# A two-layer mixer and expert trunk on one core: one layer's modulations computed on VectorE, S5 weights prepared later, the list check earlier, a new order

## The chip, the cores and the metric

The kernel runs on one core of one Trainium2 chip. The metric is the device time of one execution in microseconds (us); of several executions the median is given. Times of single instructions come from one execution that the hardware profiler recorded. PE is TensorE's matmul, PEld its weight load, DVE is VectorE, ACT is ScalarE, POOL is GpSimd, SP is SyncE, which here only issues DMAs.

## What is computed

512 tokens of width 1024 pass two layers. Each layer has a mixer and a mixture of experts:

```
mod = silu(c) @ ada_w[l] + ada_b[l]           # 6 vectors of 1024: shift, scale, gate, twice
h   = rms_norm(x) * (1 + sc1) + sh1
z   = h @ w_in[l]                             # columns go to four mixers
mix = concat(rwkv7(z), norm(s5(z)), norm(mla(z)), norm(rglru(z)))
x   = x + gt1 * (mix @ w_out[l])
h2  = rms_norm(x) * (1 + sc2) + sh2
x   = x + gt2 * moe(h2)                       # 32 experts, 2 per token: (silu(h2@w1) * (h2@w3)) @ w2
```

All of it is float32. `c` is one vector, so `mod` is a product of a vector with a 1024 x 6144 matrix: 24 MB of weights are read per layer for it. The experts' weights are 32 x 6 MB = 192 MB per layer, each read once.

## The kernel before

**Recording and planning.** The code does not issue instructions as it runs. `Rec` records each operation (so in the trace almost all of them have one line, L277), and `Rec.plan` then puts them in an order for each engine: it is a list scheduler with a cost per operation, limited by how many buffers of each kind there are. A step's `boost` adds to its priority. The tables `STEPS` (mixer steps, one string per layer, name and boost) and `MOE` (one tuple per layer: spacing of the experts and an offset for each of their stages) give these. Each engine runs its instructions strictly in the order that comes out.

**Names.** A tile's name is the part of the program that made it; a leading `q` is a PSUM tile. `ada` is the modulations, `z` the input norm and projection, `rw` and `rwc` RWKV, `s` S5, `mla` attention, `lru` the RG-LRU, `wo` the output projection and the running `x`, `n` the second norm and routing. Of the experts `moe_s` is the token list of a pair, `moe_g` the gathered tokens, `moe_h` the hidden layer, `moe_o` the outputs, and `moe_c` the combination, which adds them to `x` (tiles `wo`). `ct` is the constants, `pk` packed parameters, `r` the ring.

**Weights.** All large weights arrive by DMAs that SP issues in order. Ring tiles `r` hold 1 MB each, and there are six. Expert weights go partly into smaller tiles of 256 KB that the mixer uses for other things (`moe_h<-moe_w`, `moe_o<-moe_w`, called part tiles here); the list `OWN` says which of a layer's numbered loads do. The weights of the first experts can so arrive while the mixer still runs.

**Modulations.** `mod_chunk` handles 512 of the 6144 columns (chunks A0 to A11 for layer 0, A12 to A23 for layer 1; all 24 run before the end of layer 0's mixer). A chunk loads 2 MB into two ring tiles and issues 8 matmuls with `cond` (silu of `c`, padded with zero columns) as the stationary operand and 512 columns of weights moving: the 1024 inputs are 8 groups of 128 partitions, and four column groups of the PE array take a matmul each. `mod_cols` and `mod_rows` gather the four partial sums with small matmuls (`qada<-ct,ada`, `qada<-ada,ct`), and add the bias.

**S5 weights.** `s5w` computes layer 1's S5 matrices (powers, weights, frame; mostly VectorE with some matmuls `qs`) beside layer 0's experts. It is recorded after all experts with a very low priority, and may start once the first pair's tokens are gathered.

**Experts.** They run in 16 pairs, 64 slots per expert. Per pair: list, gather (a GpSimd DMA, transposes on PE, scaling on VectorE), hidden layer, outputs, combine. `outputs` scales the result on VectorE, rounds it on ScalarE (`oh`) and forms the remainder `ol` on GpSimd, so that `combine` can add both parts by matmuls with a 0/1 matrix.

**List check.** After the last pair's combine, `overflow` puts in a check: every engine reads whether an expert got more than 64 tokens, and branches (L2145 to L2167). With these inputs the branch is never taken. The planner treats it as a border that no recorded operation crosses.

**RWKV tiles.** `tile_a` builds a tile's decay matrices. Two products with the same stationary `Q` (against `BH`, 64 columns, and `AB`, 32 columns) are issued as separate matmuls.

Of the kernel before, what the change touches and what calls it, by code (L numbers as in the profile page):

```python
# [105 lines left out]
class Rec:  # L106


    def __init__(self, tc):
        self.tc, self.real = tc, tc.nc  # L110
        self.ops, self.hist, self.tag, self.cap = [], {}, {}, {}
        self.marks = []
        self.boost = 0.0
        self.after = None
        self.step = None
        self.stream = "main"
        self.nc = _Proxy(self)
# [9 lines left out]
    def add(self, eng, name, a, kw):  # L127
# [153 lines left out]
    def plan(self, seq, verbose=False):  # L281
# [28 lines left out]
        dma_free = hw_free = 0.0  # L310
# [16 lines left out]
        for si, (lo, hi) in enumerate(self.parts):  # L327
# [7 lines left out]
            while len(order) < hi - lo:  # L335
# [68 lines left out]
                free[e] = s + c  # L404
# [79 lines left out]
def _mk_consts():  # L484
# [25 lines left out]
    _const("selb", (p[:, None] % 32 == np.arange(4)[None, :]) | (p[:, None] == 4 + np.arange(4)[None, :]))  # L510
    _const("zero", np.zeros((1, 1)))
# [143 lines left out]
class Rwkv:  # L655
# [94 lines left out]
    def tile_a(self, tt):  # L750
# [26 lines left out]
        BH = k.s([128, 4, 64])  # L777
# [16 lines left out]
        ab2 = AB.rearrange("p h a t -> p h (a t)")  # L794
        nc.vector.tensor_mul(ab2, ab2, n2[:, tt, :, None].to_broadcast([128, 4, 2 * CH]))
# [47 lines left out]
        for at_, n, lhs, rhs, st in ((0, 64, lambda h, cs: Q[cs, h, 0], lambda h, cs: BH[cs, h], True),  # L843
                                     (64, CH, lambda h, cs: Q[cs, h, 0], lambda h, cs: AB[cs, h, 1], False),
# [11 lines left out]
        self.t[tt] = (CS, HS, AB, AK, Q, VB, MB, N, GT)  # L856

    def tile_b(self, tt, out):
# [5 lines left out]
        for hp in range(2):  # L864
            for h, i, ps_ in HS[hp::2]:
                for m, x in ((AB, Q[:, h, 1]), (AK, VB[:, h])):
                    for cs in CS:
                        nc.tensor.matmul(yp[hp][cs, i], m[cs, h, 1], x[cs], start=i == 0 and m is AB, stop=False,
                                         skip_group_check=True)
# [584 lines left out]
def positions(k, pool, pos):  # L1454
# [9 lines left out]
    for tt in range(4):  # L1464
# [15 lines left out]
MOE = [(133, 63, -18, 106, -205, -65, 19), (45, 33, 33, 167, 329, 46, 18)]  # L1480
# [134 lines left out]
class Trunk:  # L1615
# [115 lines left out]
    def mod_cols(self, l, g):  # L1731
# [5 lines left out]
        for j in range(4):  # L1737
            nc.tensor.matmul(pc[:, j], part[:, j::4], k.c("sel")[:, :g.n], start=True, stop=True)
# [6 lines left out]
    def mod_rows(self, l, g):  # L1745
# [8 lines left out]
        nc.tensor.matmul(pb[0:4], k.c("selb"), part, start=True, stop=True)  # L1754
# [289 lines left out]
    def hidden(self, xg, e, w13, gs, hd):  # L2044
# [4 lines left out]
        for j in range(8):  # L2049
# [3 lines left out]
            for q, ps in ((0, ph[os_]), (1, ph[es])):  # L2053
                nc.tensor.matmul(ps, xg[j][:, es], w[q][jj][0], start=j == 0, stop=j == 7, skip_group_check=True)
# [4 lines left out]
    def outputs(self, l, hd, w2):  # L2059
# [8 lines left out]
        for j in range(4):  # L2068
            if j % 2 == 0:
                w = [w2(e, j // 2) for e in range(2)]  # L2070
            for h in range(2):
                for e in range(2):
                    es = slice(64 * e, 64 * e + 64)
                    nc.tensor.matmul(po[h][es], hT[:, j, es], w[e][j % 2][h], start=j == 0,
                                     stop=j == 3, skip_group_check=True)
        out = []
        for h in range(2):
# [3 lines left out]
            self.split(of, nc.scalar, nc.gpsimd, oh, ol)  # L2081
# [13 lines left out]
    def moe(self, l, X, Z, E):  # L2095
# [8 lines left out]
        for e in range(0, E_N, 2):  # L2104
# [4 lines left out]
            if e == 0:  # L2109
                self.first = self.R.last.idx  # L2110
# [200 lines left out]
```

## Time and profile before

| | us |
|---|---|
| median of 3 executions (lowest, highest) | 1909.92 (1909.84, 1913.19) |
| profiled execution, its own time | 1914.02 |
| its span from first to last instruction | 1912.3 |
| PE busy | 1728.6 (90%) |
| DVE busy | 1002.4 (52%) |
| ACT busy | 430.3 (22%) |
| POOL busy | 145.5 (8%) |

The granted clock of TensorE was 0.938 of full speed over the span. The span has these stages, by the names in the timeline: a start of some 40 us; the mixer of layer 0 to about 458; its experts to about 1020; the mixer of layer 1 to about 1390; its experts to 1904; and the final stores. "Busy" of an engine in a window counts only instructions that compute. DMA is the share of the core's 16 DMA engines' time, GB/s what they moved. Idle time of PE is named after what ended it ("<-DMA" a transfer, "<-DVE z" a VectorE result).

### The profile page before, as it was taken

How to read it: one execution, taken by the hardware profiler on the slowest of the kernel's cores; microseconds unless marked ns; L12 is line 12 of the kernel's file. 1: busy time of each engine (PE TensorE's matmuls, PEld its weight loads, DVE VectorE, ACT ScalarE, POOL GpSimd, SP SyncE). 2: the span in 40 equal slices, each digit the busy share in tenths (PEclk: the TensorE clock that was granted, in tenths of full speed). 3: DMA queues.
4: the chain of work that ended last, by engine and by line, in shares of the span. 5: the costliest groups of instructions: out<-in, count | busy, mean ns of one | idle time of the engine just before them, and what ended most of it. 6: DMA issues, size and time to landing. Idle time of an engine off the chain costs nothing. (4 is left out here: it accounts for less than half of the span.)

```text
span 1912.3 us, 32680 instructions
## 1 busy us (share of the span) xinstructions
PE 1728.6 (90%) x12548; PEld 925.6 (48%) x12549; DVE 1002.4 (52%) x3448; ACT 430.3 (22%) x887; POOL 145.5 (8%) x136
## 2 busy tenths in 40 slices
PE   5989998897999998899897999999879998899987
PEld 2745655676344443333335765677734443333332
DVE  7966555658875543122226486677744374222312
ACT  3513234532011101010104253435301100100100
POOL 0000000001101220010100000000021141010101
PEclk9998998697999999999998999699989999999999
DMA  9384555044999988999995212114289999999996
GB/s 364 134 316 172 199 174 197 27 141 130 340 404 401 378 305 293 347 402 404 405 388 222 88 49 69 54 48 141 95 302 402 403 399 392 404 402 403 402 402 265
DMA packets 177397, 519.36 MB, mean 272 GB/s; under 512 B 18368, under 2 KB 20928, under 8 KB 147792
## 3 DMA queue, kind: packets, MB, share of 16 engines
q1 hardware_dynamic: 160272, 481.27, 66.3%
q10 hardware_dynamic: 11840, 19.13, 3.0%
q0 software_dynamic: 5120, 16.78, 2.6%
q8 instruction: 101, 1.65, 0.4%
q14 instruction: 64, 0.52, 0.1%
HBM read 508.71 MB, written 8.40 MB: 270 GB/s over the span
## 5 line engine op out<-in xcount | busy, mean ns | idle before, releaser
L277 PE MATMUL qmoe_h<-r,moe_g 128*64 128x512 f32 x1168 | 471.7, 608 | 17.5 <-DMA r<-moe_w 14.9
L277 PE MATMUL qmoe_h<-moe_h,moe_g 128*64 128x512 f32 x880 | 393.9, 604 | 1.5 <-DMA moe_h<-moe_w 1.5
L277 PE MATMUL qmoe_o<-r,moe_o 128*64 128x512 f32 x544 | 239.1, 647 | 16.1 <-ACT moe_o L277 14.6
L277 PEld LDWEIGHTS qmoe_h<-r,moe_g 128*64 128x64 f32 x1168 | 134.6, 139 | 201.1 <-issue 171.2
L277 DVE TENSOR_TENSOR wo<-qmoe_c,wo 128x512 f32<-128x512 f32 x256 | 159.9, 683 | 131.7 <-PE qmoe_c L277 131.6
L277 PE MATMUL qmoe_o<-moe_o,moe_o 128*64 128x512 f32 x480 | 224.9, 641 | 0.1
L277 PE MATMUL qz<-z,z 128*128 128x512 f32 (+1 forms) x816 | 216.1, 414 | 8.2 <-DVE lru L277 3.4
L277 PEld LDWEIGHTS qz<-z,z 128*128 128x128 f32 (+1 forms) x816 | 151.3, 192 | 60.3 <-issue 16.2
L277 ACT ACTIVATE moe_h<-qmoe_h 64x512 f32<-64x512 f32 x64 | 37.9, 592 | 570.5 <-PE qmoe_h L277 484.3
L277 DVE SCALAR_TENSOR_TENSOR moe_g<-qmoe_h,moe_s,moe_h 64x512 f32<-64x512 f32 x64 | 47.9, 749 | 221.6 <-ACT moe_h L277 218.8
L277 PEld LDWEIGHTS qmoe_h<-moe_h,moe_g 128*64 128x64 f32 x880 | 110.1, 138 | 104.3 <-issue 75.4
L277 PE MATMUL qmoe_c<-moe_o,moe_g 128*128 128x512 f32 x512 | 145.5, 415 | 13.7 <-ACT moe_o L277 7.9
L277 DVE TENSOR_TENSOR moe_o<-qmoe_o,moe 128x512 f32<-128x512 f32 x64 | 44.1, 691 | 211.6 <-PE qmoe_o L277 188.1
L277 POOL TENSOR_TENSOR moe_o<-moe_o,moe_o 128x512 fp32r<-128x512 f32 x64 | 82.6, 1298 | 799.4 <-ACT moe_o L277 641.1
L277 PEld LDWEIGHTS qmoe_c<-moe_o,moe_g 128*128 128x128 f32 x512 | 89.3, 188 | 101.3 <-issue 37.8
L277 PEld LDWEIGHTS qmoe_o<-r,moe_o 128*64 128x64 f32 x544 | 69.6, 147 | 137.6 <-issue 110.4
L277 POOL DMA_INDIRECT moe_g<-xn,moe_s x64 | 61.7, 964 | 946.5 <-DVE moe_s L277 857.4
L277 PE MATMUL qrw<-rw,rw 32*32 32x32 f32 (+6 forms) x4128 | 113.9, 220 | 7.3 <-DVE rw L277 2.0
L277 DVE TENSOR_SCALAR moe_g<-qmoe_g,A,B 128x128 f32<-128x128 f32 x256 | 85.5, 404 | 60.5 <-PE qmoe_g L277 47.1
L277 PEld LDWEIGHTS qrw<-rw,rw 32*32 32x32 f32 (+3 forms) x4128 | 82.0, 118 | 66.1 <-issue 26.8
L277 DVE TENSOR_TENSOR s<-s,s 128x128 f32<-128x128 f32 (+8 forms) x446 | 103.3, 290 | 3.7 <-ACT s L277 2.8
L277 ACT CAST moe_o<-moe_o 128x512 fp32r<-128x512 f32 x64 | 39.6, 619 | 282.6 <-DVE moe_o L277 209.3
(225 smaller groups left out, 2051.2 us busy)
## 6 DMA issues: line engine op xcount, KB each, us to landing
r<-moe_w SPq DMA_DIRECT2D x214, 1024.0 KB
moe_h<-moe_w SPq DMA_DIRECT2D x440, 256.0 KB
moe_o<-moe_w SPq DMA_DIRECT2D x240, 256.0 KB
r<-ada_w SPq DMA_DIRECT2D x48, 1024.0 KB
r<-w_in SPq DMA_DIRECT2D x16, 1024.0 KB
r<-w_out SPq DMA_DIRECT2D x8, 1024.0 KB
xn<-n ACTq DMA_DIRECT2D x16, 256.0 KB
z<-x SPq DMA_DIRECT2D x8, 256.0 KB
```

The costliest lines, as they stand in the source:

```text
L277: getattr(getattr(self.real, o.eng), o.fn)(*o.a, **o.kw)
```

## The change

1. Layer 1's modulations: a chunk's 8 matmuls become 8 VectorE operations 128x512 (one multiplication by a per-partition scalar, seven multiply-and-adds) into a tile `acc`, and one matmul with a matrix of ones sums the 128 partitions. Layer 0's chunks stay as they were.
2. `ada_w` is laid out on the host so that each partition's 8 KB of a ring tile lie together (four pieces of 2 KB before).
3. `tile_a`: `BH` and `AB` lie side by side in `BA`, and one matmul of 96 columns takes the place of one of 64 and one of 32; a ScalarE copy and a split VectorE operation per tile fill `BA`.
4. `s5w` is recorded after experts 18, 20 and 22, each part not before the combine of that pair, with that step's priority.
5. The list check stands ahead of the last pair's combine, in both layers, and the last pair's `ol` is formed on VectorE.
6. `OWN` sends loads 6 to 15 (instead of 6 to 11) and every odd one after them to part tiles.
7. The final stores go half to SP, half to ACT.
8. The planner takes the DMAs as free from 2.5 us on, does not hold SP at the list check, and lets a pair of matmuls wait for both weight tiles at once (`also`); `STEPS` and `MOE` have new numbers, so that all steps stand in a new order.

```diff
@@ Rec.plan
-        dma_free = hw_free = 0.0
+        dma_free, hw_free = 2500.0, 0.0
...
-                free[e] = s + c
+                if o.a is not None:
+                    free[e] = s + c
@@ tile_a
-        BH = k.s([128, 4, 64])
+        BA = k.s([128, 4, 64 + 2 * CH])
+        BH = BA[:, :, :64]
...
+        nc.vector.tensor_mul(AB[:, :, 0], AB[:, :, 0], n4)
+        nc.vector.tensor_mul(BA[:, :, 64:64 + CH], AB[:, :, 1], n4)
+        nc.scalar.copy(BA[:, :, 64 + CH:], AK[:, :, 1])
...
-        for at_, n, lhs, rhs, st in ((0, 64, lambda h, cs: Q[cs, h, 0], lambda h, cs: BH[cs, h], True),
-                                     (64, CH, lambda h, cs: Q[cs, h, 0], lambda h, cs: AB[cs, h, 1], False),
+        for at_, n, lhs, rhs, st in ((0, 64 + CH, lambda h, cs: Q[cs, h, 0], lambda h, cs: BA[cs, h, :64 + CH], True),
@@ tables
-MOE = [(133, 63, -18, 106, -205, -65, 19), (45, 33, 33, 167, 329, 46, 18)]
+MOE = [(134, 188, -31, 184, -340, -50, 357), (66, -306, 138, 370, 114, 93, -14)]
-OWN = [[i for i in range(6, 170) if i < 12 or i % 2] for _ in range(2)]
+OWN = [[i for i in range(6, 170) if i < 16 or i % 2] for _ in range(2)]
-STEPS = {0: """A0:7 A1:86 L1:72 A2:44 A3:194 G0 L4:56 G1 n:3 z1:-21 L0:104 L2:-12 A12 Z4:2 A8:-11 A9:3 w0:5 w1:2 A4:6 A5 A10:-4
+STEPS = {0: """A0:144 w0:3 L1:1 A2:-12 A3:22 A1:38 G0:-15 L2 G1:395 n:-30 z1:58 k:-37 L4:88 L0:23 Z4:-44 z2:203 A4:-21 w2:-362
...
@@ mod_chunk
+        w = self.early.pop((l, c), None) or self.load_ada(l, c)
+        if l:
+            acc = self.k.s([128, 512])
+            for h in range(2):
+                for q in range(4):
+                    col = self.cond[:, 4 * h + q, 3:4]
+                    if h + q == 0:
+                        nc.vector.tensor_scalar(acc, w[h][:, q], col, None, op0=OP.mult)
+                    else:
+                        nc.vector.scalar_tensor_tensor(acc, w[h][:, q], col, acc, op0=OP.mult, op1=OP.add)
+            g.acc[r] = acc
+            if r ^ 1 in g.acc:
+                if g.ps is None:
+                    g.ps = self.k.ps("d")
+                for n in (r & 2, r | 1):
+                    nc.tensor.matmul(g.ps[32 * n:32 * n + 32], self.k.c("ones")[:, :32], g.acc[n], start=True, stop=True)
+            return
@@ outputs
-            self.split(of, nc.scalar, nc.gpsimd, oh, ol)
+            self.split(of, nc.scalar, lo, oh, ol)
@@ moe
+            last = e == E_N - 2
+            out = self.outputs(l, hd, lambda q, h: self.load_w2(l, e + q, h), nc.vector if last else nc.gpsimd)
+            if last:
+                self.R.step, self.R.boost = None, 0.0
+                self.overflow(l, X, Z, G)
             stage(e, 5)
             self.combine(X, PT, out)
+            if e in between:
+                stage(e, 5)
+                self.R.after = self.R.last.idx
+                between[e]()
+                self.R.after = None
@@ store_x
-                self.nc.scalar.dma_start(dst[tt * 128:tt * 128 + 128, 512 * h:512 * h + 512], X[tt][h])
+                eng = self.nc.sync if h and dst is self.out else self.nc.scalar
+                eng.dma_start(dst[tt * 128:tt * 128 + 128, 512 * h:512 * h + 512], X[tt][h])
@@ build
-                self.R.after, self.R.boost = self.first, -4e6
-                for n in range(3 * (l + 1 < layers)):
-                    self.s5w(l + 1, n)
-                self.R.after, self.R.boost = None, 0.0
-                self.overflow(l, X, Z, G)
+                between = {18+2*n: partial(self.s5w, l + 1, n) for n in range(3)} if l + 1 < layers else {}
+                self.moe(l, X, Z, E, G, between)
@@ pack
+    ada = np.ascontiguousarray(np.asarray(a["ada_w"]).reshape(2, 2, 128, 4, 12, 512).transpose(0, 4, 1, 2, 3, 5))
```

The first place is layer 0's mixer. On PE before, modulation matmuls (`qada<-r,cond`) with their waits for ring DMAs stand between projection matmuls (`qz`) and attention (`qmla`):

```order
L277 MATMUL qada_184<-r_357,cond 32x512 [waits DMAHW4_49]
L277 MATMUL qada_184<-r_357,cond 32x512 x3
L277 MATMUL qada_184<-r_358,cond 32x512 [waits DMAHW5_49]
L277 MATMUL qada_184<-r_358,cond 32x512 x3
L277 MATMUL qada_184<-r_359,cond 32x512 [waits DMAHW6_49]
L277 MATMUL qada_184<-r_359,cond 32x512 x3
L277 MATMUL qada_184<-r_360,cond 32x512 [waits DMAHW7_49]
L277 MATMUL qada_184<-r_360,cond 32x512 x3
L277 MATMUL qada_284<-r_361,cond 32x512 [waits DMAHW0_49]
```

On PE after, at a place among the RWKV matmuls (`qrw`), one matmul with ones (`qada<-ada,ct`) is left of a chunk, and waits for VectorE:

```order
L279 MATMUL qrw_537<-rw_503,rw_532 64x96 [waits PE_49]
L279 MATMUL qrw_537<-rw_503,rw_532 64x96 x3
L279 MATMUL qrw_537<-rw_532,rw_503 64x64 x4
L279 MATMUL qrw_537<-rw_501,rw_504 64x64 x4
L279 MATMUL qada_294<-ada_333,ct 32x512 [waits DVE_49]
L279 MATMUL qz_411<-z_181,z_409 128x512
L279 MATMUL qz_411<-z_185,z_409 128x512
```

On DVE after, in the same stretch, the sums `ada` stand between RWKV operations (`rw`) and the splits of `w_in` (`z<-r`):

```order
L279 TENSOR_TENSOR rw_523<-qrw_522,ct 128x128 [waits PE_49]
L279 TENSOR_TENSOR rw_495<-qrw_494,rw_346 128x512
L279 TENSOR_SCALAR ada_333<-r_331,cond 128x512 [waits DMAHW4_49]
L279 TENSOR_SCALAR rw_495<-rw_495,pk_71 128x512 [waits DVE_49]
L279 STREAM_TRANSPOSE rw_526<-qrw_524 128x128 [waits Activation_49]
L279 SCALAR_TENSOR_TENSOR ada_333<-r_331,cond,ada_333 128x512 [waits DVE_49]
L279 TENSOR_TENSOR rw_528<-qrw_527,ct 128x128 [waits PE_49]
L279 TENSOR_TENSOR rw_503<-qrw_502,rw_496 128x4x64 [waits PE_49]
L279 SCALAR_TENSOR_TENSOR ada_333<-r_331,cond,ada_333 128x512 [waits DVE_49]
L279 TENSOR_TENSOR z_409<-r_327,z_407 128x512
L279 SCALAR_TENSOR_TENSOR ada_333<-r_331,cond,ada_333 128x512 [waits DVE_49]
```

So the sums share VectorE's queue with the chain on which the RWKV matmuls wait; the waits for ring DMAs moved with them.

The second place is layer 0's experts. On PE before, the S5 matmuls (`qs`) stand among the output matmuls of the seventh pair (`qmoe_o`) and the transposes of the last pairs' gathered tokens (`qmoe_g`):

```order
L277 MATMUL qmoe_g_1903<-ct,moe_g_1901 128x128 [waits DMASW4_49,DVE_49,PE_49]
L277 MATMUL qmoe_g_1903<-ct,moe_g_1901 128x128 x3
L277 MATMUL qs_2298<-s_2255,s_2273 32x32 [waits DVE_49,PE_49]
L277 MATMUL qs_2298<-s_2255,s_2273 32x32 x2
L277 MATMUL qmoe_o_1675<-r_1682,moe_o_1674 64x512 [waits DMAHW0_49]
L277 MATMUL qmoe_o_1676<-r_1682,moe_o_1674 64x512
L277 MATMUL qmoe_o_1675<-moe_o_1683,moe_o_1674 64x512 [waits DMAHW1_49]
L277 MATMUL qmoe_o_1675<-r_1682,moe_o_1674 64x512
L277 MATMUL qmoe_o_1676<-moe_o_1684,moe_o_1674 64x512 [waits DMAHW2_49]
```

On PE after, they stand inside the hidden layer (`qmoe_h`) of the twelfth pair, with waits on VectorE:

```order
L279 MATMUL qmoe_h_2057<-moe_h_2062,moe_g_2052 64x512 [waits DMAHW7_49]
L279 MATMUL qmoe_h_2057<-r_2063,moe_g_2054 64x512 [waits DMAHW0_49]
L279 MATMUL qs_2008<-s_1916,s_1934 32x32 [waits DVE_49]
L279 MATMUL qs_2008<-s_1916,s_1934 32x32 x3
L279 MATMUL qs_2008<-s_2007,s_1935 32x32 [waits DVE_49]
L279 MATMUL qs_2008<-s_2007,s_1935 32x32 x3
L279 MATMUL qs_2008<-s_1916,s_1936 32x32 x4
L279 MATMUL qs_2008<-s_2007,s_1937 32x32 x4
L279 MATMUL qs_2024<-s_1916,s_1934 32x32 [waits DVE_49]
L279 MATMUL qs_2024<-s_1916,s_1934 32x32 x3
```

The number of `qs` matmuls is the same. The last `qmoe_g` stands ahead of the sixth pair's outputs now, and the VectorE operations of `s5w`, which before began beside the first pairs, follow the combine of the tenth.

The third place is the end of layer 0's experts. On PE before, the last combine (`qmoe_c`) is followed by the read of the list count:

```order
L277 MATMUL qmoe_c_2245<-moe_o_2241,moe_g_2217 128x512 [waits Pool_49]
L277 MATMUL qmoe_c_2247<-moe_o_2241,moe_g_2217 128x512
L277 MATMUL qmoe_c_2249<-moe_o_2241,moe_g_2217 128x512
L277 MATMUL qmoe_c_2251<-moe_o_2241,moe_g_2217 128x512
L2145 TENSOR_LOAD cnt_85 [waits DVE_49]
L2146 COMPARE_AND_BRANCH
```

On PE after, the first row is the check's last branch, and the last combine follows it:

```order
L2187 UNCONDITIONAL_BRANCH [waits PE_49,PE_sequencer_49]
L279 MATMUL qmoe_c_2382<-moe_o_2379,moe_g_2353 128x512 [waits DVE_49,Activation_49]
L279 MATMUL qmoe_c_2382<-moe_o_2380,moe_g_2353 128x512
L279 MATMUL qmoe_c_2384<-moe_o_2379,moe_g_2353 128x512 [waits DVE_49,PE_49]
L279 MATMUL qmoe_c_2384<-moe_o_2380,moe_g_2353 128x512
L279 MATMUL qmoe_c_2386<-moe_o_2379,moe_g_2353 128x512
L279 MATMUL qmoe_c_2386<-moe_o_2380,moe_g_2353 128x512
```

What stood ahead of the border (combine, and on DVE the sums into `wo`) stands behind it, so that operations of the next layer's mixer can be mixed with it.

## Rows read from the trace of the kernel before

**Rows 1.** The page's first part: engine, busy us (share of the span) xinstructions.

```profile
PE 1728.6 (90%) x12548; PEld 925.6 (48%) x12549; DVE 1002.4 (52%) x3448; ACT 430.3 (22%) x887; POOL 145.5 (8%) x136
```

**Rows 2.** Windows by stage: length, busy per engine (x instructions), granted clock, DMA share, GB/s.

```profile
core 0: us, PE busy (x) PEld busy (x) DVE busy (x) ACT busy (x) POOL busy (x), PEclk, DMA share, GB/s
40.00:455.00 415.00, 391.49 (x4326) 260.21 (x4323) 267.15 (x1008) 156.76 (x334) 0.00 (x0) 0.92 0.49 172
1025.00:1385.00 360.00, 335.94 (x3868) 252.62 (x3868) 256.10 (x934) 151.30 (x331) 0.00 (x0) 0.90 0.26 92
485.00:690.00 205.00, 197.81 (x909) 81.54 (x907) 135.93 (x527) 20.24 (x35) 31.00 (x27) 0.99 1.02 389
690.00:800.00 110.00, 96.88 (x454) 41.22 (x451) 38.86 (x83) 11.55 (x24) 14.36 (x13) 0.95 0.83 290
800.00:1005.00 205.00, 184.89 (x732) 70.69 (x729) 47.39 (x73) 19.22 (x32) 15.32 (x12) 0.98 1.02 399
1410.00:1890.00 480.00, 443.85 (x1910) 181.89 (x1908) 165.51 (x352) 46.24 (x77) 59.08 (x52) 0.96 1.03 401
```

**Rows 3.** Groups of PE's and DVE's instructions by form: count, busy us, mean ns, idle before.

```profile
L277 PE MATMUL qada<-r,cond 128*32 128x512 f32 x384 | 69.1, 671 | 27.0 <-DMA r<-ada_w 13.6 <-ACT cond L277 13.3
...
L277 PE MATMUL qrw<-rw,rw 32*64 32x32 f32 x256 | 13.7, 216 | 0.0
...
L277 DVE SCALAR_TENSOR_TENSOR rw<-rw,pk,rw 128x512 f32<-128x512 f32 x4 | 3.0, 740 | 0.0
...
L277 DVE TENSOR_SCALAR rw<-rw,pk,rw 128x512 f32<-128x512 f32 x4 | 2.2, 543 | 1.2 <-PE qs L277 1.2
```

**Rows 4.** PE's waits in layer 0's mixer: total us, times, longest.

```profile
PE qada L277 <- DMA r<-ada_w: 10.0, 7, 5.0
PE qrw L277 <- issue: 1.9, 2, 1.5
```

**Rows 5.** Windows of 10 us in layer 0's experts, columns as in rows 2.

```profile
690.00:700.00 10.00, 10.00 (x42) 3.39 (x39) 1.93 (x6) 0.00 (x0) 2.59 (x3) 0.78 0.59 200
740.00:750.00 10.00, 8.36 (x26) 3.38 (x27) 1.80 (x3) 1.24 (x2) 2.56 (x2) 1.00 0.61 218
770.00:780.00 10.00, 6.03 (x22) 2.40 (x24) 0.76 (x1) 1.18 (x2) 0.00 (x0) 0.98 1.00 371
```

**Rows 6.** The same for instructions of the S5 tiles alone (PE: matmuls that read them).

```profile
500.00:520.00 20.00, 0.00 (x0) 0.00 (x0) 12.77 (x89) 0.42 (x2) 1.00 1.02 379
680.00:740.00 60.00, 5.89 (x144) 4.06 (x144) 0.00 (x0) 4.30 (x12) 0.94 0.82 292
```

**Rows 7.** SP's timeline ahead of the two expert stages: start, us, DMAs.

```profile
419.83 23.76 SPq L277 DMA_DIRECT2D moe_o<-moe_w  x16
481.65 0.33 SPq L277 DMA_DIRECT2D r<-moe_w  x1
...
1317.30 42.32 SPq L277 DMA_DIRECT2D moe_o<-moe_w  x16
1402.61 0.33 SPq L277 DMA_DIRECT2D r<-moe_w  x1
```

**Rows 8.** Timeline of all engines where layer 0's experts end: start, us, [idle before <-releaser].

```profile
1015.14 2.54 POOL L277 TENSOR_TENSOR moe_o<-moe_o,moe_o 128x512 fp32r<-128x512 f32 x2 [29.02 <-ACT moe_o L277]
...
1017.03 4.92 DVE L277 TENSOR_TENSOR wo<-qmoe_c,wo 128x512 f32<-128x512 f32 x8 [1.77 <-PE qmoe_c L277]
...
1019.63 8.49 SPq L277 DMA_DIRECT2D r<-w_in  x6
...
1027.12 1.96 PE L277 MATMUL qz<-ct,z 128*128 128x128 f32 x8 [7.62 <-DVE z L277]
```

**Rows 9.** Timeline of the last 20 us, columns as in rows 8.

```profile
1899.18 1.29 POOL L277 TENSOR_TENSOR moe_o<-moe_o,moe_o 128x512 fp32r<-128x512 f32 x1 [2.22 <-ACTq L2146]
...
1901.06 2.48 DVE L277 TENSOR_TENSOR wo<-qmoe_c,wo 128x512 f32<-128x512 f32 x4 [0.22 <-PE qmoe_c L277]
1903.64 4.53 ACTq L277 DMA_DIRECT2D out<-wo  x8
```

More of the change, by code (lines that the diff above doesn't have):

```diff
@@ L114, in __init__ @@
         self.after = None
+        self.also = ()
         self.step = None
@@ L137, in add @@
         rd += [x.ap for x in ins if isinstance(x, bass.IndirectOffsetOnAxis)]
+        rd += self.also
         if name == "matmul" and not kw.get("start", True):
@@ L867, in tile_b @@
                     for cs in CS:
-                        nc.tensor.matmul(yp[hp][cs, i], m[cs, h, 1], x[cs], start=i == 0 and m is AB, stop=False,
+                        nc.tensor.matmul(yp[hp][cs, i], m[cs, h], x[cs], start=i == 0 and m is AB, stop=False,
                                          skip_group_check=True)
@@ L1683, in load_ada @@
     def load_ada(self, l, c):
-        w = self.a["ada_w"][l].rearrange("(h p j) n -> h p j n", h=2, j=4)
-        return [self.ring(w[h, :, :, c * 512:c * 512 + 512], (4, 512)) for h in range(2)]
+        return [self.ring(self.a["ada_w"][l, c, h], (4, 512)) for h in range(2)]
     def load_win(self, l, q):
@@ L1737, in mod_cols @@
         for j in range(4):
-            nc.tensor.matmul(pc[:, j], part[:, j::4], k.c("sel")[:, :g.n], start=True, stop=True)
+            nc.tensor.matmul(pc[:, j], part[:, j::4], k.c("par" if l else "sel")[:, :g.n], start=True, stop=True)
         for r, (c, out, scale) in enumerate(g.out):
@@ L1753, in mod_rows @@
         pb = k.ps("d")
-        nc.tensor.matmul(pb[0:4], k.c("selb"), part, start=True, stop=True)
+        nc.tensor.matmul(pb[0:4], k.c("parb" if l else "selb"), part, start=True, stop=True)
         row = k.s([4, 512])
@@ L2053, in hidden @@
             for q, ps in ((0, ph[os_]), (1, ph[es])):
+                self.R.also = [w[1][jj][0]] if q == 0 else ()
                 nc.tensor.matmul(ps, xg[j][:, es], w[q][jj][0], start=j == 0, stop=j == 7, skip_group_check=True)
@@ L2073, in outputs @@
                     es = slice(64 * e, 64 * e + 64)
+                    self.R.also = [w[1][j % 2][h]] if e == 0 else ()
                     nc.tensor.matmul(po[h][es], hT[:, j, es], w[e][j % 2][h], start=j == 0,
@@ L2093, in combine, with moe @@
                 nc.vector.tensor_tensor(X[tt][h], ps, X[tt][h], op=OP.add)
-    def moe(self, l, X, Z, E):
+    def moe(self, l, X, Z, E, G, between):
+        nc = self.nc
         self.stream(f"moe{l}")
@@ L2108, in moe @@
             PT, xg = self.gather(l, tok, idx)
-            if e == 0:
-                self.first = self.R.last.idx
             hd = self.k.s([128, 512])
@@ L2135, in direct @@
         k = self.k
-        old = (self.nc, k.nc, k.sp, k.pp, self.live)
+        old = (self.nc, k.nc, k.sp, k.pp, self.live, self.own)
         self.nc = k.nc = self.R.real
-        k.sp, k.pp, self.live = self._Direct(self.sp, self.bufs), self._Direct(self.pp, self.pbufs), True
+        k.sp, k.pp, self.live, self.own = self._Direct(self.sp, self.bufs), self._Direct(self.pp, self.pbufs), True, []
         fn()
-        self.nc, k.nc, k.sp, k.pp, self.live = old
+        self.nc, k.nc, k.sp, k.pp, self.live, self.own = old
+        self.R.also = ()
     def over(self, l, X, Z, G):
@@ L2172, in over @@
                             self.hidden(xg, q, w13, gs, hd)
-                        out = self.outputs(l, hd, w2)
+                        out = self.outputs(l, hd, w2, nc.vector)
                         self.combine(X, PT, out)
@@ L2205, in setup @@
         nc.gpsimd.memset(self.cond, 0.0)
+        self.R.boost = 1e7
         nc.scalar.activation(self.cond[:, :, 3], ct, AF.Silu)
+        self.R.boost = 0.0
         self.cos, self.sin = positions(k, self.cp, a["pos"])
@@ L2225, in mods @@
             g = Group()
-            g.out, g.n = out, len(out)
+            g.out, g.n, g.ps, g.acc = out, len(out), None, {}
             chunks += [partial(self.mod_chunk, l, x[0], g, r) for r, x in enumerate(out)]
```

37 lines of the change are left out of this document (18 added, 19 removed).

## The prediction

> **What bounds the kernel now.** I read the page's first part, then a table of windows by stage, then PE's waits and groups inside each stage, and last the timeline at the two seams. The first part shows PE busy 90% of the span, DVE 52%, ACT 22%, POOL 8% [rows 1]. This is an average over stages with different limits, which the windows take apart [rows 2].
>
> In layer 0's mixer (40 to 455) PE is busy 391.5 of 415 us, DVE 267.2, and the DMAs at a share of 0.49. In layer 1's mixer (1025 to 1385) PE is busy 335.9 of 360. The two mixers differ mainly by the 24 modulation chunks, and the time differs as PE's work does: 55.6 us of PE, 55 us of span. So a mixer is bound by PE, with some 24 us of waits in each.
>
> The experts are another matter. From 1410 to 1890 the DMAs run at a share of 1.03 and 401 GB/s. A pair's weights are 12 x 1,048,576 = 12.58 MB, so 31.4 us at that rate; the 6.5 pairs that 800 to 1005 holds at this pace cost PE 184.9 us, 28.4 each [rows 2]. So experts are bound by DMA where nothing disturbs them. In layer 0 something does: from 690 to 800 only 290 GB/s flow, so 110 x (1 - 290/401) = 30.4 us of transfer are lost. [...] Layer 1's experts, which have no S5 weights beside them, show no such dip at 401 GB/s.
>
> **The change part by part.** The durations are from the profiled execution, 1914.0 us with a span of 1912.3; the median of the runs is 1909.9, 4.1 below it.
>
> *Modulations on VectorE.* The `qada<-r,cond` records are 384 with 69.1 us for both layers [rows 3]; half go: -34.6 us of PE. In their place come 12 ones-matmuls, 24 records of the same form. With four side by side, as now, one costs 69.1/384 = 0.18 us, so 4.3 in all; alone 0.671, so 16.1. They come two at a time: I take 8. DVE gets 84 multiply-and-adds at 0.740 and 12 multiplications at 0.543 (the same operations on SBUF tiles of 128x512): 62.2 + 6.5 = 68.7 us [rows 3]. DVE's idle time in the stage is 415 - 267 = 148 us [rows 2], which hides them if they fall into it. DVE would then be busy 336 of some 400 us, 84%, and its queue is in order: a sum in front of an operation on which the RWKV matmuls wait delays PE by up to 0.74 us. Waits for the ring move too: PE waits 10.0 us for `ada_w` in 7 places [rows 4], and in the second half of them DVE will stand in its stead, with rw operations and splits of `w_in` queued behind.
>
> *`tile_a`.* The 32-column matmuls (256 records, 13.7 us, so 6.9 per layer [rows 3]) go; the 96-column form that takes them in is not in the trace. Between nothing gained and 6.9 per layer I take 3.4. The 8 ScalarE copies lie in ACT's idle time (157 of 415 us busy [rows 2]).
>
> Together PE loses 34.6 - 8 + 3.4 = 30 us of work in layer 0's mixer. The gain in time lies between -35 (all of it, and half of the 10 us of waits) and a loss of 39 (68.7 of sums fully on the path, less 30). I take -14, about half of PE's gain, because DVE at 84% in order cannot hide everything. Layer 1's mixer: -3 (0 to -7).
>
> *S5 weights later.* In layer 0's experts, S5 takes DVE 12.8 of 20 us at 500 to 520, early, when lists and gathers of all pairs also want DVE; its matmuls fall on PE at 680 to 740 with 5.9 us [rows 6], beside the last gathers: the dip. From 485 to 690 DVE is busy 135.9 of 205 us and PE 197.8; from 800 to 1005 DVE is busy only 47.4 and PE has 20 us free [rows 2]. The change puts S5 there, behind all gathers. If the stage then looks like layer 1's, the 30.4 us come back; if the dip only moves, nothing. PE's late work has to be done in any case and is 96.5% busy ahead of the dip, so I take -19.
>
> *Deeper prefetch.* SP's part loads end at 443.6 and 1359.6, and its next ring load is issued at 481.65 and 1402.61 [rows 7]: 38 and 43 us without weights. 16 more part tiles are 4.2 MB, 10.5 us at 401 GB/s, in each layer. All of it would give -21. But at the start of the experts PE, at 96.5%, is as much the limit as the DMAs, so weights that lie ready are worth less: -6 (0 to -21). If the mixer holds the tiles longer, SP waits at them and the loads queued behind wait too; that end is 0, since SP stands still there today.
>
> *List check earlier.* At the seam GpSimd's two remainders take 2.54 us, the sums 4.92, SP's `w_in` loads come at 1019.63 after the last combine, and the first matmul of the next layer at 1027.12 waits on DVE [rows 8]. Remainders on DVE cost some 0.7 each. The loads can leave sooner, but the norm needs the sums in any case, so I take -2 (0 to -7). The added wait on DVE is behind the last scaling, with only the combine queued after it.
>
> *End.* Eight store issues take ACT 4.53 us in a row; in two queues 2.3 less. A remainder of 1.29 us on GpSimd is on the last chain, about 0.6 less on DVE [rows 9]. I take -3 (-1 to -5).
>
> *`ada_w`'s layout, the order.* PE's waits for `ada_w` bound the first at 0 to -5 together with the above; I take 0. The new order has no price of its own in the trace; PE's idle time in the mixers, some 24 us each, bounds what it can give, and I count none.
>
> Sum: -14 - 3 - 19 - 6 - 2 - 3 = -47, so 1867 against the profiled execution and 1863 against the median. I forecast 1865.
>
> **Rivals.**
>
> *VectorE eats the gain of the mixer.* For it: 84% busy, in order. Against it: 148 us idle now, and sums are not urgent. Then -14 is 0: 1879.
>
> *The dip only moves.* S5's matmuls on PE wait for DVE inside a hidden layer, and PE's queue behind them waits too. For it: 5.9 us of PE and its waits come in a stage with only 20 us of PE's idle time. Against it: DVE is nearly free there. Then -19 is 0: 1884.
>
> [...]
>
> *Slower: VectorE's queue becomes the path.* In layer 0's mixer nearly every sum stands ahead of an operation that PE awaits, and the sums' waits for the ring (10 us as PE had) hold DVE. Then 68.7 + 10 - 30 = +49 in place of -14: 1865 + 63 = 1928. It decides from +35 in this stage on, that is, when over 55 of the 68.7 us with the waits are on the path.
>
> *All ends at their best.* Mixer -35, dip -30, prefetch -21: 1865 - 21 - 11 - 15 = 1818.
>
> **How the numbers follow.** Forecast 0.42, VectorE eats the gain 0.14, the dip moves 0.12, the clock 0.07, all at their best 0.12, slower 0.10, and 0.03 that losses through the new order just cancel the gains. A difference of 0.2% (3.8 us) is about what a measurement of this kernel can tell from none. Slower has 0.10, no change 0.05 (the 0.03 and the edge of the slower case), faster 0.85. The range reaches from 1832, between forecast and best case, to 1898, above the rivals that cost one term or both (1865 + 14 + 19 = 1898); it leaves out the slower case and half of the best.
>
> **What would show it.** In layer 0's mixer, PE's busy time near 361 us over a stage some 14 us shorter; DVE near 336. If PE waits on DVE `rw` for more than 20 us there, the first or the slower rival holds. In layer 0's experts, windows of 10 us at 400 GB/s throughout, as in layer 1's; a dip where `qs` runs says that it moved. SP's pause before each expert stage begins with 4.2 MB more landed. At the seam the first `qz` comes 10.1 us after the start of the last sums today [rows 8]; it should come some 8 after it. The prediction is wrong if the mixer of layer 0 grows, or if neither expert stage gets shorter.

## The result and the profile after

The changed kernel takes 1858.46 us (median of 4, 1857.69 to 1869.05); before took 1909.88 beside it (median of 4, 1905.98 to 1913.19). By the medians that is 51 us less. The ratio is 0.9744, 95% interval 0.9705 to 0.9784, which makes it 49 us less, between 41 and 56. I forecast 1865, with 1832 to 1898 as the range. The total was near; the terms were not all, and one cause was not in the list at all, so that the nearness is in part luck.

Between the starts and ends of named matmuls in the two profiled executions (spans 1912.3 and 1856.6 us) the stages take:

| stage, us | before | after | moved | forecast |
|---|---|---|---|---|
| start and layer 0's mixer, to the last `qn` | 465.8 | 442.8 | -23.0 | -14 |
| `qn` to the first `qmoe_h`, both layers | 20.3 | 22.6 | +2.3 | |
| layer 0's experts, to the end of the last `qmoe_o` | 538.5 | 515.2 | -23.3 | -19, and part of -6 |
| from there to layer 1's first `qz` | 12.7 | 18.4 | +5.7 | -2 |
| layer 1's mixer | 357.6 | 350.2 | -7.4 | -3 |
| layer 1's experts | 502.8 | 493.2 | -9.6 | part of -6 |
| combine, sums, stores | 14.6 | 14.1 | -0.5 | -3 |

The moves add up to -55.8, more than the 51 of the medians, since the profiled execution of before took 1914.0, 4.1 above its median. A stage also varies from one profiled execution to the next: in the runs below that leave a stage's order and work alone, layer 0's mixer takes 462.1 to 467.9 us with before's order and 436.8 to 442.8 with the changed one, layer 0's experts 530.8 to 538.5 and 515.2 to 519.3. A few us in one stage of one trace therefore show nothing.

First the page's busy times, then the windows of the stages, as in [rows 1, 2]. PE lost 55 us, DVE gained 60.

```profile
PE 1673.4 (90%) x12124; PEld 900.2 (48%) x12125; DVE 1062.0 (57%) x3556; ACT 427.1 (23%) x891; POOL 139.3 (8%) x132
```

```profile
core 0: us, PE busy (x) PEld busy (x) DVE busy (x) ACT busy (x) POOL busy (x), PEclk, DMA share, GB/s
40.00:440.00 400.00, 378.25 (x4061) 260.76 (x4053) 332.25 (x1169) 156.27 (x339) 0.00 (x0) 0.90 0.51 189
1000.00:1340.00 340.00, 314.39 (x3702) 237.81 (x3700) 242.24 (x855) 136.74 (x306) 0.00 (x0) 0.93 0.26 89
...
660.00:770.00 110.00, 99.18 (x429) 38.09 (x426) 26.65 (x41) 11.81 (x20) 8.91 (x7) 0.97 1.03 416
770.00:970.00 200.00, 179.47 (x832) 68.28 (x831) 95.39 (x396) 22.20 (x44) 14.46 (x12) 0.97 0.92 361
...
900.00:910.00 10.00, 10.00 (x42) 4.79 (x42) 2.29 (x4) 0.89 (x2) 1.29 (x1) 1.00 0.64 243
```

In layer 0's mixer DVE is busy 332 of 400 us, as forecast (336), and PE 378 (361 forecast); the clock is 0.90. The stretch that ran at 290 GB/s in the middle of the experts [rows 2, 5] has 416 now. That is more than the 401 GB/s at which before ran undisturbed, and nothing in the prediction accounts for it.

The groups of PE and DVE by form, to be held against [rows 3]:

```profile
L279 DVE SCALAR_TENSOR_TENSOR ada<-r,cond,ada 128x512 f32<-128x512 f32 x84 | 60.5, 741 | 0.0
L279 DVE TENSOR_SCALAR ada<-r,cond 128x512 f32<-128x512 f32 x12 | 5.7, 475 | 1.8 <-PE qz L279 1.8
...
L279 PE MATMUL qada<-r,cond 128*32 128x512 f32 x192 | 33.2, 699 | 16.1 <-DMA r<-ada_w 16.1
L279 PE MATMUL qrw<-rw,rw 32*64 32x64 f32 x512 | 24.0, 238 | 0.0
L279 PE MATMUL qrw<-rw,rw 32*64 32x96 f32 x256 | 20.6, 277 | 1.3 <-DVE rw L279 0.8 <-ACT rw L279 0.6
...
L279 PE MATMUL qada<-ada,ct 128*32 128x512 f32 x24 | 13.2, 679 | 0.0
```

The sums cost DVE 66.2 us (forecast 68.7), the removed matmuls were 35.9 (34.6), the ones-matmuls are 13.2 (8).

PE's largest waits in that mixer (40 to 440), where [rows 4] had 10.0 us for `ada_w`. There is none for `ada_w` now, whose 16.1 us above lie ahead of 40, and none for the sums `ada` among the first:

```profile
PE qrw L279 <- DVE rw L279: 5.0, 5, 1.8
PE qz L279 <- ACT rw L279: 3.4, 1, 3.4
```

Instructions of the S5 tiles alone in layer 0's experts (columns as in [rows 6]). S5 now runs from 760 to 880 beside transfers at 380 to 415 GB/s, and the late low stretch (205 GB/s) has none of it:

```profile
780.00:800.00 20.00, 0.00 (x0) 0.00 (x0) 10.99 (x80) 0.42 (x2) 0.83 1.01 393
820.00:840.00 20.00, 2.66 (x76) 2.06 (x76) 11.24 (x37) 3.59 (x11) 1.00 1.03 415
900.00:920.00 20.00, 0.00 (x0) 0.00 (x0) 0.00 (x0) 0.00 (x0) 1.00 0.57 205
```

In the late stretch PE is full (10.00 of 10 us from 900 to 910, above) and SP waits for it to free ring tiles (from 870 to 960 36.1 us for `qmoe_h` and 26.7 for `qmoe_o`): the last 22 loads all go to the ring. The SP rows at the start answer to [rows 7]: 16 more part loads end at 429.3, and SP still stands until 459.67.

```profile
417.14 12.20 SPq L279 DMA_DIRECT2D moe_h<-moe_w  x16
459.67 0.33 SPq L279 DMA_DIRECT2D r<-moe_w  x1
...
891.83 63.43 SPq L279 DMA_DIRECT2D r<-moe_w  x22
```

The seam between the layers, as in [rows 8]. The loads of `w_in` leave at once after the last `qmoe_o` (ended 969.28). But PE's combine waits 3.09 us until DVE is past the check, and DVE mixes sums with splits that wait for casts and transfers (the first casts 3.39 us for `w_in`, the first splits 3.31 for the casts):

```profile
969.40 3.12 SPq L279 DMA_DIRECT2D r<-w_in  x6
...
971.00 0.69 DVE L279 TENSOR_TENSOR moe_o<-moe_o,moe_o 128x512 fp32r<-128x512 f32 x1 [0.73 <-ACT moe_o L279]
...
972.38 5.51 PE L279 MATMUL qmoe_c<-moe_o,moe_g 128*128 128x512 f32 x16 [3.09 <-DVEq L2187]
...
975.00 1.29 DVE L279 TENSOR_TENSOR z<-r,z 128x512 fp32r<-128x512 f32 x2 [3.31 <-ACT z L279]
...
987.69 3.11 PE L279 MATMUL qz<-ct,z 128*128 128x128 f32 x14 [9.80 <-DVE z L279]
...
997.92 5.30 PE L279 MATMUL qz<-z,z 128*32 128x512 f32 x21 [0.33 <-ACT z L279]
```

In before the combine began before the last pair's remainders were formed, and the twelve matmuls behind its first four waited only 0.18 us for GpSimd's:

```profile
1015.12 1.19 PE L277 MATMUL qmoe_c<-moe_o,moe_g 128*128 128x512 f32 x4 [0.65 <-ACT moe_o L277]
...
1016.49 3.02 PE L277 MATMUL qmoe_c<-moe_o,moe_g 128*128 128x512 f32 x12 [0.18 <-POOL moe_o L277]
```

In the changed kernel all sixteen stand behind the check, and so behind the last remainder, which DVE ends at 971.69. From the last `qmoe_o` to the end of the combine it takes 8.6 us instead of 5.0, and from there to the first `qz` 9.8 instead of 7.6. In the other traces the two are 4.4 to 5.1 and 7.6 us with before's order, 8.6 to 9.8 and 9.3 to 10.1 with the changed one where the seam was left alone.

And the end, as in [rows 9]. The stores' issue is shorter, and the combine waits 2.87 at the check; from the last `qmoe_o` to its end it takes 6.8 us instead of 4.1, and from there to the end of the span 7.4 instead of 10.5:

```profile
1845.33 3.89 PE L279 MATMUL qmoe_c<-moe_o,moe_g 128*128 128x512 f32 x16 [2.87 <-DVEq L2187]
...
1846.79 5.68 SPq L279 DMA_DIRECT2D out<-wo  x4
...
1849.04 3.08 DVE L279 TENSOR_TENSOR wo<-qmoe_c,wo 128x512 f32<-128x512 f32 x5 [0.44 <-PE qmoe_c L279]
1849.76 2.13 ACTq L279 DMA_DIRECT2D out<-wo  x4
```

### The profile page after: what moved, and what is told of

The parts are those of the page before. It is cut to its first block, busy times and chain, and to the rows that moved or that the text cites. A ratio compares the mean times of both kernels' runs of the same rounds, so it can differ in the third digit from the quotient of the medians.

```text
span 1856.6 us, 31976 instructions
## 1 busy us (share of the span) xinstructions
PE 1673.4 (90%) x12124; PEld 900.2 (48%) x12125; DVE 1062.0 (57%) x3556; ACT 427.1 (23%) x891; POOL 139.3 (8%) x132
## 5 line engine op out<-in xcount | busy, mean ns | idle before, releaser
L279 PE MATMUL qmoe_h<-r,moe_g 128*64 128x512 f32 x1136 | 442.8, 603 | 2.1 <-DMA r<-moe_w 2.1
L279 PE MATMUL qmoe_o<-r,moe_o 128*64 128x512 f32 x544 | 239.1, 646 | 14.2 <-ACT moe_o L279 14.1
L279 PEld LDWEIGHTS qmoe_h<-r,moe_g 128*64 128x64 f32 x1136 | 130.0, 138 | 200.7 <-issue 183.8
L279 PE MATMUL qz<-z,z 128*128 128x512 f32 (+1 forms) x816 | 209.7, 406 | 5.3 <-ACT rw L279 3.4
L279 PEld LDWEIGHTS qz<-z,z 128*128 128x128 f32 (+1 forms) x816 | 147.1, 186 | 59.7 <-issue 10.4
L279 PEld LDWEIGHTS qmoe_h<-moe_h,moe_g 128*64 128x64 f32 x912 | 114.8, 138 | 78.0 <-issue 61.9
L279 POOL TENSOR_TENSOR moe_o<-moe_o,moe_o 128x512 fp32r<-128x512 f32 x60 | 76.5, 1283 | 698.3 <-ACT moe_o L279 511.0
L279 PE MATMUL qrw<-rw,rw 32*32 32x32 f32 (+7 forms) x3872 | 112.5, 231 | 16.8 <-DVE rw L279 6.4
L279 PEld LDWEIGHTS qrw<-rw,rw 32*32 32x32 f32 (+4 forms) x3872 | 82.0, 124 | 58.1 <-issue 18.0
```

The source lines that it names most:

```text
L279: getattr(getattr(self.real, o.eng), o.fn)(*o.a, **o.kw)
```

## The experiments

Theory M: the mixer's gain is PE work moved into VectorE's idle time. Theory O: it is the new order. Theory S: S5's place removes the dip. The rest came up on the way.

### One part undone or done, planned anew

**Modulations back on PE.** The same is done where the constants `par` and `parb` are chosen.

```diff
-        if l:
+        if l > 1:
```

> The changed kernel with one part undone: layer 1's modulations as matmuls on PE again, all else (tables too) as changed. Theory M (the mixer's gain is PE work moved into VectorE's idle time): layer 0's mixer grows by 15 to 30 us, the time is 1875 to 1890. Theory O (the gain is the new order of the steps): it stays within 5 us of 1858. A rival in between: the plan was made for the sums on VectorE, so that PE's extra work also spoils the order, above 1890.

Measured: 1971.2 us, ratio to before 1.0271 (1.0219 to 1.0323). Layer 0's mixer takes 528.8 us instead of 442.8; PE is busy 432 of 485 us there at a clock of 0.83.

**Only the modulations moved, in before.** `mod_chunk`, `par` and `parb` as changed, all else as before.

```diff
-        for h in range(2):
-            for q in range(4):
-                nc.tensor.matmul(g.ps[32 * q:32 * q + 32], ...
+        if l:
+            acc = ...                          # as in the change
```

> The kernel before with one part done: layer 1's modulations summed on VectorE, all else as before. Theory M: layer 0's mixer is 14 to 22 us shorter, the time 1888 to 1896. Theory O: with the old order VectorE's sums land in the path and the time is 1905 or more. Its rate of weights from 1410 to 1890 also tells whether the 415 GB/s of the changed kernel's profile (403 before) belong to the kernel: then it shows 403, else about 415 on the same chip.

Measured: 1986.96 us, ratio 1.0373 (1.0327 to 1.0419); the mixer takes 513.6 us, 48 more than before. The transfers run at 415 GB/s from 1700 to 1800, where before has 403; so the higher rate is not the changed kernel's alone. The waits of PE in the mixer show the mechanism of the slower rival:

```profile
PE qada L277 <- DVE ada L277: 22.9, 3, 13.4
PE qrw L277 <- DVE rw L277: 8.0, 7, 2.5
```

The ones-matmul stands in PE's queue ahead of work that is ready, and waits for late sums.

**The changed code with the old tables.**

```diff
-MOE = [(134, 188, ...
+MOE = [(133, 63, ...                          # STEPS too, as before
```

> The changed kernel with the numbers of STEPS and MOE of before. Theory O: most of the 51 us are lost, 1890 or more. Theory M with S (S5 late removes the dip): 1860 to 1875.

Measured: 2020.98 us, ratio 1.0508 (1.0431 to 1.0585); mixers of 533.3 and 410.1 us.

**S5 early in the changed kernel.**

```diff
-                between = {18+2*n: partial(self.s5w, l + 1, n) for n in range(3)} ...
+                self.R.after, self.R.boost = self.first, -4e6   # as before, ahead of the check
```

> The changed kernel with S5's weights where they were before: lowest priority, from the first pair's gather on. Theory S: the dip in layer 0's experts comes back ahead of pair 8, +12 to +25 us, 1870 to 1883. Rival (the dip only moved, as the trace after shows 243 and 167 GB/s at 900 to 920): within 5 us of 1858.

Measured: 1915.18 us, ratio 0.9991 (0.9964 to 1.0018). Layer 0's experts take 544.5 us, 29.3 more, and the dip is back around the S5 matmuls:

```profile
670.00:710.00 40.00, 3.25 (x37) 2.33 (x36) 0.00 (x0) 4.28 (x12) 0.96 0.73 252
```

But layer 1's mixer, of which nothing was edited, takes 375.5 us instead of 350.2. So these four do not price parts: any edit makes the planner find another order, and an order found for other code loses more than the part is worth. Neither M nor O came out. By the ratios to before's 1916.33 us beside them, the modulations alone are 71 us slower, the whole change with the old tables 97, and the change without the modulations 52. The following runs therefore keep the order of the changed kernel, or of before, and alter one thing in it.

### In a fixed order: what the sums and PE's work cost

**Before, unchanged.** No edit.

> The kernel before, unchanged, profiled once more. If the rate of weights is a matter of the run and not of the kernel, the windows of layer 1's experts show about 415 GB/s instead of 401, and that stage is some 6 us shorter than in the first profile (502.8 us from the first hidden-layer matmul to the last output matmul); if the rate belongs to the changed kernel, 401 GB/s again.

Measured: 1912.83 us; 399 GB/s from 1410 to 1890 and 504.5 us for the stage, on the chip on which the next three kernels move 416 GB/s from 1600 to 1700, where this one moves 399. So the rate belongs to the kernel.

**Sums left out.**

```diff
+                if _sum(o) and o.fn == "scalar_tensor_tensor":
+                    continue
                 getattr(getattr(self.real, o.eng), o.fn)(*o.a, **o.kw)
```

> The changed kernel in its own order on every engine, with seven of the eight VectorE operations of each of layer 1's modulation chunks left out (84 multiply-and-adds, 62 us of VectorE; part of the modulations is not computed). Theory M (the sums lie in VectorE's idle time): layer 0's mixer is 0 to 8 us shorter. Rival V (VectorE eats half of the gain, as the prediction took it): 12 to 20 us shorter.

Measured: 1859.68 us, ratio 0.9732 (0.9676 to 0.9787). The mixer takes 441.3 us, 1.5 less, which is within the 436.8 to 442.8 of this order with the sums in it. DVE is busy 286 us instead of 332:

```profile
40.00:440.00 400.00, 378.67 (x4078) 261.76 (x4073) 286.10 (x1111) 158.02 (x342) 0.00 (x0) 0.91 0.51 191
```

**Sums twice.**

```diff
                 getattr(getattr(self.real, o.eng), o.fn)(*o.a, **o.kw)
+                if _sum(o) and o.fn == "scalar_tensor_tensor":
+                    self.real.vector.scalar_tensor_tensor(o.a[0], o.a[1], rec_zero(self), o.a[3], **o.kw)
```

`rec_zero` gives a column of zeros.

> The changed kernel in its own order, with each of the 84 multiply-and-adds of layer 1's modulations followed by one more of the same shape with a zero scalar: 62 us more on VectorE in layer 0's mixer, which was busy 332 of 400. Theory M: the idle time left (68 us) takes most, the mixer grows by 10 to 25 us. Rival V: the queue is full in effect, 40 to 62 us more.

Measured: 1917.33 us, ratio 1.0039 (1.0012 to 1.0066). The mixer takes 494.3 us, 51.5 more, as rival V had it and theory M did not. PE waits for the sums again, and the clock is 0.87 from 40 to 490:

```profile
PE qada L279 <- DVE ada L281: 15.7, 4, 6.2
PE qrw L279 <- DVE rw L279: 12.2, 10, 2.2
```

**PE's work put back as load.**

```diff
+                if _ones(o):
+                    self.extra = getattr(self, "extra", 0) + 1
+                    for _ in range(2 + self.extra % 2):
+                        getattr(getattr(self.real, o.eng), o.fn)(*o.a, **o.kw)
```

> The changed kernel in its own order, with 30 more matmuls 32x512 on PE, two or three in front of each ones-matmul of layer 1's modulations: 60 records of some 0.59 us, 35 us of PE, as much as the change took away. Theory M (PE sets the mixer's end): layer 0's mixer grows by 28 to 38 us. Rival: 15 us or less, if VectorE or the transfers set the end now.

Measured: 1883.84 us, ratio 0.9851 (0.9791 to 0.9911). The added matmuls measure 30.2 us, not 35. The mixer takes 468.1 us, 25.3 more, somewhat under theory M's 28 to 38. The whole stage in before, in the changed kernel, and in this run (columns as in [rows 2]):

```profile
0.00:465.80 465.80, 416.41 (x4440) 274.31 (x4441) 306.56 (x1324) 173.85 (x373) 0.85 (x7) 0.92 0.53 187
```

```profile
0.00:442.80 442.80, 400.51 (x4144) 270.22 (x4145) 365.17 (x1424) 170.67 (x374) 0.85 (x7) 0.90 0.55 206
```

```profile
0.00:468.10 468.10, 420.09 (x4204) 273.40 (x4205) 364.76 (x1424) 170.99 (x374) 0.85 (x7) 0.93 0.53 194
```

So in this order the sums cost nothing that can be told from none, and PE's load about 25 us. With as much of PE's work as before (420.1 us busy against 416.4) the new order is no faster there than before (468.1 against 465.8): in layer 0's mixer the gain is PE's work and not the order. Theory M holds for this stage, in this order alone. The first 60 us of sums fall into idle time, the next 63 cost 51.5.

### Where 404 and 417 GB/s come from

**32 bytes more, in before and in the changed kernel.**

```diff
         self.ct = self.fixed([128, CP.n], F32, "ct")
+        self.pad = self.fixed([128, 8], F32, "pad")
```

> The kernel before with nothing changed but one unused tile of 32 bytes per partition behind the constants, so that every tile behind it, ring and part tiles too, lies 32 bytes further on; the order is the same on every engine. In before they start at 28640 bytes and so on, in the changed kernel (whose constants are 32 bytes longer) at 28672, a multiple of 512. Theory A (the place of the tiles makes the difference between 404 and 417 GB/s): 416 GB/s, each expert stage 6 to 14 us shorter, the time 1885 to 1900. Rival (the rate comes from the order, the layout of ada_w or the chip's state): 404 GB/s and 1908 to 1914.

> The changed kernel with the same unused tile of 32 bytes, which moves its ring and part tiles off the multiple of 512; the order is the same. Theory A: 404 GB/s, each expert stage 5 to 12 us longer, the time 1868 to 1882. Rival: 417 GB/s and 1855 to 1862.

Measured: before with the pad 1900.08 us, ratio 0.9927 (0.9898 to 0.9956), 12 us less by the medians; layer 1's experts take 497.3 us instead of 504.5. The changed kernel with it 1877.43 us, ratio 0.9801 (0.9767 to 0.9836), against 0.9744 without: some 11 us more; its layer 1's experts take 503.6 us instead of 493.2. In layer 0's experts the pad shows no difference beyond the spread of the traces. The window from 1600 to 1700 of before, of before with the pad, of the changed kernel, and of the changed kernel with the pad:

```profile
1600.00:1700.00 100.00, 90.32 (x384) 33.55 (x380) 27.63 (x49) 9.88 (x17) 7.58 (x6) 0.97 1.03 399
```

```profile
1600.00:1700.00 100.00, 89.96 (x376) 33.30 (x374) 24.37 (x38) 10.20 (x17) 7.59 (x6) 0.95 1.03 414
```

```profile
1600.00:1700.00 100.00, 92.00 (x380) 33.82 (x377) 26.55 (x41) 9.07 (x16) 7.59 (x6) 0.95 1.03 416
```

```profile
1600.00:1700.00 100.00, 91.51 (x379) 35.27 (x377) 24.85 (x38) 10.25 (x17) 9.25 (x8) 0.98 1.03 403
```

The DMA share is 1.03 in all four: the engines are full, and move 3 to 4% more where the tiles lie at the multiple. The run of before with the modulations alone, which has the two constants and the old layout of `ada_w`, fits with its 415 GB/s. The two new constants `par` and `parb` are 8 columns, 32 bytes; they moved the tiles there by chance.

### Prefetch and seam in a fixed order

**The 16 part loads behind the first ring load.**

```diff
+                r67 = big[6]                       # the first ring load behind the part loads
...
+                late = q[r67 - 16:r67]
+                q[r67 - 16:r67 + 1] = [q[r67]] + late
```

> The changed kernel in its own order but for SP: in both layers the 16 part loads (4.2 MB) that the longer list added ahead of the experts are issued right behind the first ring load that waits for the experts' start. Theory P (weights lying ready are worth their transfer time): 8 to 12 us longer in each expert stage, 1875 to 1883. The prediction's size (3 each): 1861 to 1867. Rival (PE is the limit there anyway): within 3 us of 1858.

Measured: 1860.64 us, ratio 0.9734 (0.9697 to 0.9770); experts of 515.8 and 493.0 us, within 0.6 of the changed kernel's. The deeper prefetch is worth nothing that these runs can tell. PE is busy 79.6 of the 80 us from 480 to 560 with it, and 79.6 from 476 to 556 without it.

**The sums ahead of the splits at the seam.**

```diff
...
+                first = min(i for i, o in enumerate(q) if o.fn == "tensor_tensor")
+                sums = [q[i] for i in w]           # the eight sums of the last pair
+                rest = [o for i, o in enumerate(q) if i not in w]
+                qs["vector"] = rest[:first] + sums + rest[first:]
```

> The changed kernel in its own order but for VectorE behind the first list check: the eight sums of the last pair stand ahead of the splits of layer 1's w_in (in the changed kernel they stand between them, and each split waits for a transfer and a cast). Theory Q (the sums are late because VectorE waits in order): the first qz comes 5 to 8 us sooner, and the time is 1850 to 1854, below both kernels. Rival (the splits are needed as soon): within 2 us of 1858, as the main qz matmuls then wait for the splits.

Measured: 1864.92 us, ratio 0.9749 (0.9717 to 0.9780). The sums run in one piece, and yet the first `qz` comes later, 21.5 us after the last `qmoe_o` instead of 18.4, since the splits are now in front of the norm:

```profile
978.03 4.88 DVE L292 TENSOR_TENSOR wo<-qmoe_c,wo 128x512 f32<-128x512 f32 x8 [5.08 <-PE qmoe_c L292]
...
992.06 3.32 PE L292 MATMUL qz<-ct,z 128*128 128x128 f32 x16 [12.90 <-DVE z L292]
...
1000.81 4.43 PE L292 MATMUL qz<-z,z 128*32 128x512 f32 x10 [0.17 <-ACT z L292]
```

Theory Q fell, and the rival's 2 us were not met either, though the intervals overlap. No version here beats the changed kernel clear of the intervals.

## Why the prediction was right, and where its steps were not

- *What bounds.* Right: mixers by PE (30.2 us of added load cost 25.3), experts by DMA where nothing disturbs them (a share of 1.03 from 1600 to 1700, before and after).
- *Modulations, -14 with `tile_a`.* Counts and durations were right: -35.9 and +66.2 us. The size was not: -23.0. I took half of PE's gain because DVE would be busy 84%. It was (332 of 400), but the sums cost nothing that could be measured: in this order they lie in idle time. A busy share does not tell that; the order does. PE's groups lost 35.9 - 13.2 + 3.0 = 25.7 us; its busy time in the stage fell by 15.9 (416.4 to 400.5) and its idle time by 7.1. With the old tables and a plan made anew, the rival in which VectorE's queue becomes the path came true (+48 us in the mixer); I forecast +49 for it, but had tied it to no order.
- *Ones-matmuls, `tile_a`.* 13.2 us instead of 8, so they run nearly as single ones (0.55 a record, where one alone was taken at 0.671 and four side by side at 0.18). The 96-column form saves 50.6 - 44.6 = 6.0 us over both layers, 3.0 each, against 3.4. The 50.6 are the 13.7 of [rows 3] and the 36.9 of this row of before:

```profile
L277 PE MATMUL qrw<-rw,rw 32*64 32x64 f32 x768 | 36.9, 233 | 1.8 <-DVE mla L277 0.8 <-ACT rw L277 0.5 <-ACT lru L277 0.3
```

- *Layer 1's mixer, -3.* It moved by -7.4. 3.0 of it are `tile_a`; what the rest is stays open, as nothing was tried on that stage alone.
- *S5 later, -19.* The mechanism is supported: early S5 brings the dip back (+29.3 us in that stage, but in a new plan), late S5 runs beside up to 415 GB/s. No run moved S5 in a fixed order. The stage moved by -23.3; by the other traces of the two orders it is 12 to 23. The rival in which the dip only moves is wrong in its cause: the late low stretch has no S5 in it, and SP waits there for ring tiles that a full PE holds.
- *Prefetch, -6.* Wrong: nothing. The reason that I gave for taking little (PE is as much the limit there) fits all of it: PE is full there (79.6 of 80 us) with and without the deeper prefetch.
- *List check, -2; end, -3.* Wrong in sign at the seam, +5.7. I priced the check's added wait at nothing, since only the combine is queued after it. But the whole combine then waits for the last remainder and the check, where in before it had begun ahead of the remainder: 3.6 of the 5.7 us lie between the last `qmoe_o` and the end of the combine, 2.2 behind it, where DVE mixes sums and splits. At the end the same takes 2.7 us, most of the 3.2 that come back behind the combine. That the check is the cause was read from the waits; it was not tried alone. Another 2.3 us went to the two stretches between `qn` and `qmoe_h`, for which I had no term.
- *Layer 1's experts.* -9.6 comes from the tiles' place: with the pad the stage is 503.6, before's 502.8 to 504.5, and the other traces of the changed order 493.0 to 499.8. This term was missing from the sum. It is worth some 11 to 12 us in the total, about a quarter of the gain. Without it the change would have come to some 1870, above my forecast instead of below it. The total came near because this missing term and the mixers' larger gains made up for the prefetch, the seam and the end.
- *The clock, 0.07.* That the removed matmuls lower the clock is not shown. Over the whole stage layer 0's mixer fell from 0.92 to 0.90, and PE's busy time there is 400.5 us where 390.7 were to be left (416.4 - 25.7). But other traces of the changed order show 0.90 to 0.92 with the same work, and layer 1's mixer went the other way, from 0.91 to 0.92. Whether the 9.8 us come from the clock was not tried.

## What to carry to other kernels

An order found by a search belongs to the code for which it was found: price a part with every queue held fixed, and alter only what is issued; the modulations on PE cost layer 0's mixer 86 us in a new plan, and a like load on PE 25 us in the fixed order. Work in the idle time of an engine off the path is free until that is used up, and then costs most of its length: the first 60 us cost nothing measurable here, the next 63 cost 51.5. When a stage bound by transfers changes its rate and no transfer was edited, look at where the tiles lie: 32 bytes made 414 GB/s of 399 here.

## What the runs showed of the hardware

- With the same order and the same loads, transfers from 1600 to 1700 ran at 399 GB/s in before, whose ring tiles start at 28640 bytes in a partition, and at 414 with the pad, which puts them at 28672, a multiple of 512. In the changed kernel, which has 28672 without the pad, they ran at 416, and with it, at 28704, at 403. The part tiles move by the same 32 bytes. Which multiple matters, and why, was not tried.
- In a fixed order, 60 more matmul records of 30.2 us in layer 0's mixer came with a granted clock of 0.93 over that stage, against 0.90 to 0.92 in the traces of this order with nothing added to that stage. PE's busy time there rose by 19.6 us and the stage by 25.3. That the clock made the difference is not shown.
- Seven of eight VectorE operations of 128x512 on the sums (60.5 us) could be left out of a stage in which DVE was busy 332 of 400 us, and the stage took 441.3 us, against 436.8 to 442.8 with them.
